# A two-layer diffusion backbone on one core: the norm barriers' elementwise work moved from GpSimd to VectorE, with the three sums on all partitions

## The chip, the core and the metric

The kernel runs on one core of one Trainium2 chip. A core has a tensor engine (TensorE, PE in the profile), a vector engine (VectorE, DVE), a scalar engine (ScalarE, ACT), GpSimd (POOL) and a sync engine (SyncE, SP) that issues most of the loads. The metric is the device time of one execution in microseconds (us), lower is better; three runs of the kernel before gave 1486.10, 1487.79 and 1488.62 us, median 1487.79.

## What is computed

Two layers of a diffusion backbone run over 256 latent tokens x and 256 context tokens, 1024 features each. Cut to what matters here:

```python
def rmsnorm(x, g):
    return x * rsqrt(mean(x * x, axis=-1) + EPS) * g

for l in range(2):
    h  = rmsnorm(x,  g_pre_mix) * (1 + sc1)  + sh1        # modulation from the conditioning vector
    hc = rmsnorm(xc, g_pre_mix) * (1 + scc1) + shc1
    y, y_ctx = token_mixer(h, hc)                         # four branches, gates, output projection
    x  = x + g1 * rmsnorm(y, g_post_mix)
    h2 = rmsnorm(x, g_pre_ffn) * (1 + sc2) + sh2
    x  = x + g2 * rmsnorm(conv_ffn(h2), g_post_ffn)
    # layer 0 does the same to the context; layer 1 needs it only as keys and values
```

Everything is fp32. The products are made of three passes over high and low parts (hi·hi, hi·lo, lo·hi), so each weight and each activation is split: the high part is a cast, the low part is the value minus the high part.

## The kernel before

**Layout.** Features lie on the 128 partitions, eight tiles `m` of 128 features; the tokens lie side by side, 512 columns of which 0 to 255 are context and 256 to 511 latent. The two halves are called streams (`streams`, `segs`); layer 1 keeps only the latent one in its second part. A dense product is `gemm_steps`: for each of eight feature tiles three matmuls (lines 236, 237, 238) into a bank of the accumulator memory (`pg` with three banks, `pa` with five).

**Weights.** `weights` loads a chunk into `st` through SP's queue and `parts` (line 215 the cast on ScalarE, line 217 the low part) splits it. The low part is VectorE's, but GpSimd's where `ahead`, `pool` or `held` says so: the first four feed-forward weights of layer 0 (`first_weights`), some of the next layer's (`tm_weights`), one of layer 1's output projection, and the three that follow a norm barrier. These last are `held`: `issue_after` puts their casts behind the last tile's ScalarE work and their low parts behind the last scaling. `stream` gives the feed-forward weights one after the other, two ahead of use; its first call issues three loads, its second makes their parts.

**A norm barrier.** It stands between two dense stages, since every feature of a token must be summed before the next product can begin. `post_tile` (lines 407 to 417) takes each output tile of the projection, multiplies it by its gain into `acc`, and keeps running sums of src², x·acc and acc². `post_sums` (line 428) adds these over the partitions by products with a matrix of ones: the first into one bank on all partitions, the two others into one bank, on partitions 0 to 31 and 32 to 63. `post_end` then computes 1/rms of the output and, from the three sums, 1/rms of the new residual without reading it again: `fold` (line 439) transposes 32x32 blocks so that a token's sum is one column, `rsqrt` (lines 318 to 327) does ten small steps, `unfold` (line 445) spreads the result back over the columns. The second root runs on 32 partitions; four copies (line 482) put it on all 128 before the last `unfold`. `scale` (line 515) multiplies `acc` by 1/rms, on GpSimd; `residual` (line 521) adds it to x, on VectorE but for tile 0; `modulate_steps` (lines 389 to 398) makes the next product's input: x·r on VectorE, two ScalarE activations for the high part and the modulated value, and the low part on VectorE.

**Order.** TensorE runs in the order of the trace. VectorE and ScalarE run in an order that a planner chooses from the trace's order, but `in_order` keeps the instructions inside it in theirs; in layer 1 that holds for the whole barrier. While the barrier lasts, TensorE is given fillers (`fill`, line 637): products of the next modulation, loaded by SP's queue. `closing` runs the last tiles a stream after the other, so that the first stream's norm runs beside the second stream's products. `channel` holds both barriers of a layer. After each barrier, `spill` stores x through GpSimd's DMA queue.

There are three barriers in the middle of the program: after the output projection of layer 0 (two streams), after its feed-forward half (two streams) and after the output projection of layer 1 (one stream). The last norm, at the very end, only scales, adds and stores (lines 1519 to 1521).

Of the kernel before, what the change touches and what calls it, by code (L numbers as in the profile page):

```python
# [18 lines left out]
D = 1024  # L19
KT = D // 128  # L20
SEQ = 256
# [12 lines left out]
# columns of the per-layer vector pack  # L34
# [4 lines left out]
# columns of the constant pack  # L39
# [114 lines left out]
class Net:  # L154
# [13 lines left out]
    # ---- allocation  # L168
# [27 lines left out]
    def weights(self, src, cols, ahead=False, pool=False, dve=False):  # L196
        return self.parts(self.staged(src, cols), cols, ahead, pool, dve)
# [6 lines left out]
    def parts(self, st, cols, ahead=False, pool=False, dve=False):  # L204
        """the high and the low part of weights"""
# [25 lines left out]
    def mm3_steps(self, out, pairs, n=None):  # L231
        """out = sum over pairs of (lhsT hi, lhsT lo, rhs hi, rhs lo): the three products that matter; yields columns streamed"""
# [12 lines left out]
    def gemm_steps(self, out, w, x, cols, k0=0, m=128, ms=128, off=0):  # L245
        """out[M, tokens] = w[:, k, M].T @ x[k][:, cols] over the k tiles of x"""
# [21 lines left out]
    def finish(self, f):  # L268
        """trace all that is queued up to f"""
# [4 lines left out]
    def gemm_tm(self, outs, x, ws, n, kg):  # L274
        """out[tokens, n] = x[k][:, tokens].T @ w[:, k, n] for several token tiles, kg k tiles to a chunk of weights"""
# [19 lines left out]
    def stack_q(self, dst, src, cols):  # L295
        """two heads of 64 features: dst[h] has a head's high parts on its own rows, its low parts on the other's"""
# [6 lines left out]
    def stack_k(self, hi, lo, src, cols):  # L303
        """hi[h] has a head's high parts on all rows; lo the low parts of both heads"""
# [7 lines left out]
    # ---- norms  # L312
    def rsqrt(self, v):
        """1/sqrt(v) by a step of third and one of second order from a guess of the exponent"""
        nc = self.nc
        stt, tt, ts = nc.vector.scalar_tensor_tensor, nc.vector.tensor_tensor, nc.vector.tensor_scalar
# [5 lines left out]
        ts(nh, v, -0.5, None, op0=ALU.mult)  # L322
        stt(t, e, -10.0 / 3.0, e, op0=ALU.add, op1=ALU.mult)  # L323
        stt(z, t, 5.0, s, op0=ALU.add, op1=ALU.mult)  # L324
        tt(a, z, z, op=ALU.mult)
        tt(b, a, nh, op=ALU.mult)
        stt(r, b, 1.5, z, op0=ALU.add, op1=ALU.mult)
        return r
# [9 lines left out]
    def sums(self, out, parts, n):  # L338
        """out[tokens, token tile] = sum over the features of all parts"""
# [8 lines left out]
    def squares(self, tiles, cols):  # L348
        """squares of the features' tiles, added in pairs"""
# [11 lines left out]
    def rstd(self, tiles, cols, room):  # L361
        """1/sqrt(mean of squares over the features + eps), on every partition, for the tokens of cols"""
# [20 lines left out]
    def modulate_steps(self, h, m, segs, r, Am, Bm, vector=False):  # L383
        """h[m] = x[m] * r * A + B, split; A and B are [128, KT, 2]; a generator that yields before the last step"""
# [15 lines left out]
    def post_tile(self, src, m, segs, G, more):  # L400
        """acc[m] = src * G, and what the norms need of it: sums of src^2, x * acc, acc^2"""
# [6 lines left out]
        for cs, b in segs:  # L408
            act = nc.scalar.activation(self.acc[:, m, cs], src[:, cs], AF.Identity, scale=G[:, m, b:b + 1])
        if more:  # L410
            act = nc.scalar.activation(yy, yg, AF.Square)
            (nc.gpsimd if m == KT - 1 and oc.start == self.xc0 else nc.vector).tensor_tensor(xy, self.xcols(m, oc), yg, op=ALU.mult)
# [5 lines left out]
        else:  # L418
            self.last3 = [t[:, oc] for t in new]
            if oc.stop == T:  # L420
                self.act = getattr(act, "ins", act)
                self.held = 3
# [1147 lines left out]
```

## Time and profile before

| | |
|---|---|
| time, median of three runs | 1487.79 us |
| span of the profiled execution | 1481.7 us |
| TensorE busy | 1399.2 us (94%) |
| VectorE busy | 983.1 us (66%) |
| ScalarE busy | 661.6 us (45%) |
| GpSimd busy | 131.8 us (9%) |
| mean granted TensorE clock | 0.971 |
| moved by DMA | 208 MB, 140 GB/s |

The profile is one execution; its span runs from the first to the last instruction, and the runs' times contain what lies around it. A busy share is an average over stages: what bounds one stage is read from the timeline and the waits of that stage. A group of instructions shows its count, the busy time of all and the mean of one, and behind the second bar the idle time before them. Matmuls overlap, so a busy TensorE can still hold less work than its window could. In a timeline a row is a start time, a length, the engine, the line, what is written and read, and in brackets the idle time before it with what ended it; equal neighbours are merged, with their count.

### The profile page before, as it was taken

What the parts mean: (1) busy time and instruction counts of PE and PEld (TensorE: products, weight loads), DVE (VectorE), ACT (ScalarE), POOL (GpSimd) and SP (SyncE); (2) the same over time, 40 slices, a digit from 0 to 9 for tenths busy, and PEclk for the clock granted to TensorE, in tenths of its full rate; (3) what the DMA queues carried; (4) which work ended last, traced back from release to release, by engine and by line L of the source; (5) the groups of instructions that cost most, each with busy time, mean ns of one, the idle gap of its engine ahead of it and who ended that gap; (6) DMA issues with size and microseconds to landing.
All of it is one profiled execution on the core that took longest, in us unless ns stands there. A gap on an engine that the chain in (4) does not pass through costs nothing. (4 is left out here: it accounts for less than half of the span.)

```text
span 1481.7 us, 22257 instructions
## 1 busy us (share of the span) xinstructions
PE 1399.2 (94%) x8657; PEld 1176.8 (79%) x8657; DVE 983.1 (66%) x1901; ACT 661.6 (45%) x1158; POOL 131.8 (9%) x136
## 2 busy tenths in 40 slices
PE   6999999999999979999999998699999999599996
PEld 3887777777778858878888887487889898599996
DVE  5458686646645797743554658958676876765666
ACT  3446444324434545323322335455563565455453
POOL 0200000100000270000000002700000000300000
PEclk8999999999999979999999999699999999799998
DMA  9722232442222624443344433453333467257553
GB/s 290 272 72 88 94 120 98 156 157 72 71 72 85 213 100 171 154 142 102 127 130 156 156 102 113 152 179 115 103 111 127 130 199 249 81 173 225 184 181 91
DMA packets 73418, 208.00 MB, mean 140 GB/s; under 512 B 6881, under 2 KB 24673, under 8 KB 73185
## 3 DMA queue, kind: packets, MB, share of 16 engines
q1 hardware_dynamic: 65792, 179.32, 37.8%
q0 software_dynamic: 7520, 27.27, 5.3%
q8 instruction: 68, 1.11, 0.3%
q14 instruction: 38, 0.30, 0.1%
HBM read 201.31 MB, written 5.24 MB: 139 GB/s over the span
## 5 line engine op out<-in xcount | busy, mean ns | idle before, releaser
L217 DVE TENSOR_TENSOR wl<-st,wh 128x1024 fp32r<-128x1024 f32 (+2 forms) x252 | 303.6, 1210 | 207.8 <-ACT wh L215 206.3
L215 ACT CAST wh<-st 128x1024 fp32r<-128x1024 f32 (+2 forms) x262 | 268.3, 1033 | 359.3 <-PE pg L237 192.7
L236 PE MATMUL pg<-hh,wh 128*128 128x512 f32 (+1 forms) x1136 | 402.6, 354 | 0.0
L238 PE MATMUL pg<-hh,wl 128*128 128x512 f32 (+1 forms) x1136 | 384.2, 338 | 1.3 <-DVE wl L217 1.2
L237 PE MATMUL pg<-hl,wh 128*128 128x512 f32 (+1 forms) x1136 | 383.3, 337 | 0.0
L236 PEld LDWEIGHTS pg<-hh,wh 128*128 128x128 f32 x1136 | 215.5, 190 | 31.4 <-issue 7.2
L238 PEld LDWEIGHTS pg<-hh,wl 128*128 128x128 f32 x1136 | 215.3, 190 | 25.9 <-DVE wl L217 2.3
L237 PEld LDWEIGHTS pg<-hl,wh 128*128 128x128 f32 x1136 | 215.7, 190 | 23.1 <-issue 3.1
L236 PE MATMUL pa<-hh,wh 128*128 128x256 f32 (+1 forms) x376 | 126.1, 335 | 1.1 <-ACT hh L292 1.1
L237 PE MATMUL pa<-hl,wh 128*128 128x256 f32 (+1 forms) x376 | 126.2, 336 | 0.6 <-DVE hl L293 0.6
L238 PE MATMUL pa<-hh,wl 128*128 128x256 f32 (+1 forms) x376 | 126.0, 335 | 0.0
L236 PE MATMUL pg<-u,wh 128*128 128x256 f32 (+1 forms) x350 | 120.2, 343 | 0.0
L237 PE MATMUL pg<-u,wh 128*128 128x256 f32 (+1 forms) x350 | 115.2, 329 | 0.0
L238 PE MATMUL pg<-u,wl 128*128 128x256 f32 (+1 forms) x350 | 115.1, 329 | 0.0
L237 PEld LDWEIGHTS pa<-hl,wh 128*128 128x128 f32 x376 | 71.4, 190 | 8.4 <-DVE hl L293 1.2
L236 PEld LDWEIGHTS pa<-hh,wh 128*128 128x128 f32 x376 | 71.4, 190 | 8.4 <-ACT hh L292 1.3
L238 PEld LDWEIGHTS pa<-hh,wl 128*128 128x128 f32 x376 | 71.4, 190 | 7.1
L236 PEld LDWEIGHTS pg<-u,wh 128*128 128x128 f32 x350 | 66.2, 189 | 12.9 <-issue 7.0
L237 PEld LDWEIGHTS pg<-u,wh 128*128 128x128 f32 x350 | 66.1, 189 | 6.5 <-issue 1.0
L238 PEld LDWEIGHTS pg<-u,wl 128*128 128x128 f32 x350 | 65.9, 188 | 6.6
L626 DVE SCALAR_TENSOR_TENSOR u<-u,cs,u 128x1024 f32<-128x1024 f32 x49 | 61.5, 1278 | 1.2 <-DMA u<-wmod 1.1
L818 ACT ACTIVATE pp<-pa,nbias 128x512 f32<-128x512 f32 (+1 forms) x48 | 29.5, 615 | 67.9 <-DVE nbias L816 37.2
(304 smaller groups left out, 2271.9 us busy)
## 6 DMA issues: line engine op xcount, KB each, us to landing
st<-wup SPq DMA_DIRECT2D x88, 512.0 KB, 3.7
st<-wgate SPq DMA_DIRECT2D x64, 512.0 KB, 3.6
u<-wmod SPq DMA_DIRECT2D x48, 512.0 KB, 4.7
u<-wmod POOLq DMA_DIRECT2D x32, 512.0 KB, 4.7
st<-wdn SPq DMA_DIRECT2D x32, 448.0 KB, 3.3
st<-win SPq DMA_DIRECT2D x26, 512.0 KB, 4.0
u<-wmod SPq DMA_DIRECT2D x32, 256.0 KB, 6.1
st<-wbr SPq DMA_DIRECT2D x16, 512.0 KB, 3.6
```

The source lines that it names most:

```text
L215: nc.scalar.copy(hi[:, :cols], st[:, :cols])
L217: (nc.gpsimd if (ahead or held or pool) and not dve else nc.vector).tensor_tensor(lo[:, :cols], st[:, :cols], hi.bitcast(F32)[:, :cols], o ...
L236: mm(out, ah, bh, start=i == 0, stop=False)
L237: mm(out, ah, bl, start=False, stop=False)
L238: mm(out, al, bh, start=False, stop=i == n - 1)
L626: nc.vector.scalar_tensor_tensor(t, st, self.cs[:, k, i:i + 1], t, op0=ALU.mult, op1=ALU.add)
L818: nc.scalar.activation(P[:, :n], S[:, :n], AF.Exp, bias=nb, scale=scale, accum_out=den)
```

## The change

All elementwise tensor work on GpSimd goes to VectorE: the low parts of weights, the scalings by 1/rms, the product x·acc of the last tile, the residual of tile 0 and a quarter of the last multiply-and-add. The holds on the weights after a barrier are removed with it. The three sums of a barrier go into three banks, each on all partitions, so that all three are folded and both roots are computed on all 128 partitions; the four copies are gone. `rsqrt` takes a list of functions (`room`) and calls one after each of its steps: the folds of the second and third sum are put into the first root, the spreading of 1/rms into the second, and in layer 1 also the scaling and the residual of tiles 0 and 1. `scale` and `add` of a tile are called together, tile by tile. In layer 1 tiles 0 and 1 are modulated with one activation on ScalarE and one instruction on VectorE in place of two activations. The second call of `stream` moves behind the modulation of both streams.

```diff
-        held = self.held > 0
-        self.held -= 1
-        with self.tc.issue_after(self.act) if held else nullcontext():
-            nc.scalar.copy(hi[:, :cols], st[:, :cols])
-        with self.tc.issue_after(self.res) if held else nullcontext():
-            (nc.gpsimd if (ahead or held or pool) and not dve else nc.vector).tensor_tensor(lo[:, :cols], st[:, :cols], hi.bitcast(F32)[:, :cols], op=ALU.subtract)
+        nc.scalar.copy(hi[:, :cols], st[:, :cols])
+        nc.vector.tensor_tensor(lo[:, :cols], st[:, :cols], hi.bitcast(F32)[:, :cols], op=ALU.subtract)
...
+    def rsqrt(self, v, room=()):
...
+        def step():
+            for f in room:
+                f()
+                break
+
         ts(y.bitcast(I32), v.bitcast(I32), -0.5, float(0x5f3759df), op0=ALU.mult, op1=ALU.add)
+        step()
         tt(a, y, y, op=ALU.mult)
         ts(s, y, 0.375, None, op0=ALU.mult)
+        step()
...
     def post_sums(self, parts, first):
         for i, p in parts:
-            o = self.s12[32 * i - 32:32 * i] if i else self.s0
-            self.nc.tensor.matmul(o[:, :p.shape[-1]], self.one[:, :o.shape[0]], p, start=first, stop=not first)
+            self.nc.tensor.matmul(self.s[i][:, :p.shape[-1]], self.one, p, start=first, stop=not first)
 
     def post_runs(self, segs):
-        self.s0, self.s12 = self.pa([T]), self.pa([T])
+        self.s = [self.pa([T]) for _ in self.run3]
...
         with self.in_order():
-            nc.vector.tensor_scalar(v, self.fold(self.s0, w), 1.0 / D, EPS, op0=ALU.mult, op1=ALU.add)
-            r = self.rsqrt(v)
-            self.unfold(r, self.rb[:, oc])
+            sums(0)
+            nc.vector.tensor_scalar(v, f[0], 1.0 / D, EPS, op0=ALU.mult, op1=ALU.add)
+            r = self.rsqrt(v, [lambda: None] * 3 + [lambda: sums(1), lambda: sums(2)] if more else ())
             if not more:
+                self.unfold(r, self.rb[:, oc])
                 return
-            s = self.fold(self.s12[0:64], w)
-            nc.vector.tensor_tensor(p[32:64], s[32:64], r[32:64], op=ALU.mult)
...
-            r2 = self.rsqrt(v2)
-            for i in range(4):
-                nc.vector.tensor_copy(r4[32 * i:32 * i + 32], r2)
-            self.unfold(r4, self.rx[:, oc])
+            nc.vector.tensor_tensor(p, f[2], r, op=ALU.mult)
+            nc.vector.scalar_tensor_tensor(q, f[1], 2.0, p, op0=ALU.mult, op1=ALU.add)
+            nc.vector.tensor_tensor(q, q, r, op=ALU.mult)
+            nc.vector.scalar_tensor_tensor(v2, q, 1.0 / D, v2, op0=ALU.mult, op1=ALU.add)
+            self.unfold(self.rsqrt(v2, [lambda: self.unfold(r, self.rb[:, oc]), *room]), self.rx[:, oc])
...
     def scale(self, m, segs):
         acc = self.acc[:, m, self.span(segs)]
-        ins = self.nc.gpsimd.tensor_tensor(acc, acc, self.rb[:, self.span(segs)], op=ALU.mult)
-        if m == KT - 1:
-            self.res = getattr(ins, "ins", ins)
+        self.nc.vector.tensor_tensor(acc, acc, self.rb[:, self.span(segs)], op=ALU.mult)
...
+    def residual(self, m, segs):
+        self.scale(m, segs)
+        self.add(m, segs)
...
                 if last:
-                    self.post_end([seg], True)
+                    self.post_end([seg], True, [lambda f=f, m=m: f(m, [seg]) for m in range(2) for f in (self.scale, self.add)])
                     self.fill(1.5)
-                if seg is segs[-1]:
-                    for m in range(KT):
-                        self.scale(m, [seg])
                 for m in range(KT):
                     if seg is not segs[-1] and m == 4:
                         self.post_end(segs[1:], True)
-                    if seg is segs[-1] or m >= 4:
-                        self.residual(m, [seg], last)
-                    open_steps.append(self.modulate_steps(h, m, [seg], self.rx, A, B))
+                    if m >= (2 if last else 4) or not last and seg is segs[-1]:
+                        self.residual(m, [seg])
+                    open_steps.append(self.modulate_steps(h, m, [seg], self.rx, A, B, last and m < 2))
...
-                    if seg is segs[0] and m == (KT - 1 if c0 == 0 else 0):
-                        next(self.ws)
                     if seg is segs[-1]:
                         self.spill(m, c0, c0)
+        next(self.ws)
         self.ffn(l, h, c0, not last)
...
-                on = nc.gpsimd if m == 4 else nc.vector
...
-                on.tensor_tensor(acc, acc, rb.to_broadcast([128, n, SEQ]), op=ALU.mult)
-                on.tensor_tensor(x, x, acc, op=ALU.add)
+                nc.vector.tensor_tensor(acc, acc, rb.to_broadcast([128, n, SEQ]), op=ALU.mult)
+                nc.vector.tensor_tensor(x, x, acc, op=ALU.add)
```

## Rows read from the trace of the kernel before

**Rows 1.** The page, part 1: busy time, share of the span, instructions.

```profile
PE 1399.2 (94%) x8657; PEld 1176.8 (79%) x8657; DVE 983.1 (66%) x1901; ACT 661.6 (45%) x1158; POOL 131.8 (9%) x136
```

**Rows 2.** Windows: length; busy PE, PEld, DVE, ACT, POOL; clock; DMA share; GB/s.

```profile
526.80:573.70 46.90, 37.62 (x273) 29.98 (x272) 38.82 (x104) 22.55 (x40) 26.38 (x20) 0.82 0.41 142
921.70:970.40 48.70, 32.62 (x164) 24.23 (x156) 41.72 (x110) 22.58 (x42) 33.23 (x33) 0.75 0.57 202
1255.20:1289.60 34.40, 18.91 (x165) 15.42 (x158) 26.15 (x61) 13.72 (x24) 14.68 (x14) 0.75 0.33 107
...
1275.00:1280.00 5.00, 4.12 (x17) 3.83 (x18) 4.18 (x13) 4.55 (x9) 0.80 (x1) 0.50 0.12 41
1280.00:1285.00 5.00, 5.00 (x41) 5.00 (x40) 3.85 (x11) 4.36 (x8) 0.76 (x1) 0.91 0.30 105
```

**Rows 3.** Timeline of TensorE, third barrier.

```profile
1275.37 0.58 PE L236 MATMUL pg<-hh,u 128*128 128x256 f32 x1 [13.85 <-ACT hh L392]
```

**Rows 4.** Timeline of VectorE, third barrier.

```profile
1256.34 0.45 DVE L439 STREAM_TRANSPOSE t<-pa 128x256 f32<-128x256 f32 x1 [3.26 <-PE pa L428]
...
1258.65 0.45 DVE L445 STREAM_TRANSPOSE rs<-n 128x256 f32<-128x256 f32 x1
...
1264.62 2.37 DVE L322 TENSOR_SCALAR n<-xms 32x8 f32<-32x8 f32 x1
...
1272.90 0.45 DVE L445 STREAM_TRANSPOSE rs<-nr 128x256 f32<-128x256 f32 x1
```

**Rows 5.** Timeline of GpSimd, third barrier.

```profile
1259.17 5.50 POOL L515 TENSOR_TENSOR acc<-acc,rs 128x256 f32<-128x256 f32 x8 [2.47 <-ACT wh L215]
1264.63 6.92 POOL L217 TENSOR_TENSOR wl<-st,wh 128x1024 fp32r<-128x1024 f32 x3
```

**Rows 6.** Groups of VectorE by line and form, first barrier, 519 to 567 us.

```profile
L482 DVE COPY nr<-n 32x8 f32<-32x8 f32 x8 | 7.7, 958 | 0.1
L389 DVE TENSOR_TENSOR t<-u,rs 128x256 f32<-128x256 f32 x16 | 7.1, 479 | 0.1
...
L521 DVE TENSOR_TENSOR u<-u,acc 128x256 f32<-128x256 f32 x14 | 5.7, 406 | 0.0
L417 DVE TENSOR_TENSOR t<-t,t 128x256 f32<-128x256 f32 x6 | 2.9, 477 | 0.1
...
L412 DVE TENSOR_TENSOR t<-u,acc 128x256 f32<-128x256 f32 x3 | 1.8, 587 | 0.1
```

**Rows 7.** Timeline of VectorE, first and second barrier.

```profile
519.39 0.45 DVE L439 STREAM_TRANSPOSE t<-pa 128x256 f32<-128x256 f32 x1 [4.30 <-PE pa L428]
...
531.78 5.98 DVE L482 COPY nr<-n 32x8 f32<-32x8 f32 x4
...
538.80 1.42 DVE L389 TENSOR_TENSOR t<-u,rs 128x256 f32<-128x256 f32 x4
...
565.75 0.92 DVE L398 TENSOR_TENSOR hl<-t,hh 128x256 fp32r<-128x256 f32 x2 [1.05 <-ACT t L396]
...
917.28 0.44 DVE L439 STREAM_TRANSPOSE t<-pa 128x256 f32<-128x256 f32 x1
...
948.81 6.44 DVE L482 COPY nr<-n 32x8 f32<-32x8 f32 x4
...
965.52 0.43 DVE L398 TENSOR_TENSOR hl<-t,hh 128x256 fp32r<-128x256 f32 x1
```

**Rows 8.** Groups, whole program: the split on VectorE and on GpSimd.

```profile
L217 DVE TENSOR_TENSOR wl<-st,wh 128x1024 fp32r<-128x1024 f32 (+2 forms) x252 | 303.6, 1210 | 207.8 <-ACT wh L215 206.3
...
L217 POOL TENSOR_TENSOR wl<-st,wh 128x1024 fp32r<-128x1024 f32 x8 | 18.7, 2345 | 47.8 <-ACT wh L215 47.8
```

**Rows 9.** Timeline of VectorE at the end of the program.

```profile
1472.26 2.36 DVE L1519 TENSOR_TENSOR acc<-acc,rs 128x512 f32<-128x512 f32 x2
...
1477.52 0.69 DVE L1520 TENSOR_TENSOR u<-u,acc 128x512 f32<-128x512 f32 x1
```

**Rows 10.** Timeline of VectorE at the start of the program.

```profile
45.90 4.36 DVE L394 TENSOR_SCALAR t<-t,A,mod 128x256 f32<-128x256 f32 x2 [1.22 <-ACT hh L392]
```

More of the change, by code (lines that the diff above doesn't have):

```diff
@@ L193, in pf, with weights @@
         return self.pa(shape) if self.turn else self.pg(shape)
-    def weights(self, src, cols, ahead=False, pool=False, dve=False):
-        return self.parts(self.staged(src, cols), cols, ahead, pool, dve)
+    def weights(self, src, cols, ahead=False):
+        return self.parts(self.staged(src, cols), cols, ahead)
     def staged(self, src, cols):
@@ L202, in staged, with parts @@
         return st
-    def parts(self, st, cols, ahead=False, pool=False, dve=False):
+    def parts(self, st, cols, ahead=False):
         nc = self.nc
@@ L408, in post_tile @@
         for cs, b in segs:
-            act = nc.scalar.activation(self.acc[:, m, cs], src[:, cs], AF.Identity, scale=G[:, m, b:b + 1])
+            nc.scalar.activation(self.acc[:, m, cs], src[:, cs], AF.Identity, scale=G[:, m, b:b + 1])
         if more:
-            act = nc.scalar.activation(yy, yg, AF.Square)
-            (nc.gpsimd if m == KT - 1 and oc.start == self.xc0 else nc.vector).tensor_tensor(xy, self.xcols(m, oc), yg, op=ALU.mult)
+            nc.scalar.activation(yy, yg, AF.Square)
+            nc.vector.tensor_tensor(xy, self.xcols(m, oc), yg, op=ALU.mult)
         if m == 0:
@@ L445, in unfold, with post_end @@
         self.nc.vector.transpose(o.rearrange("p (j r) -> p j r", r=32), r.unsqueeze(2).to_broadcast([128, J, 32]))
-    def post_end(self, segs, more):
+    def post_end(self, segs, more, room=()):
         nc = self.nc
@@ L454, in post_end @@
         small = lambda t: self.sm([16], t, bufs=1)[:, :J]
-        v, p, q, r4 = small("nv"), small("np"), small("nq"), small("nr")
-        v2 = self.xms[0:32, oc.start // 32:oc.stop // 32]
+        v, p, q = small("nv"), small("np"), small("nq")
+        v2 = self.xms[:, oc.start // 32:oc.stop // 32]
         parts = list(enumerate(self.last3))
@@ L468, in post_end, with sums @@
             self.fill(1.5)
+        f = [None] * 3
+        def sums(i):
+            f[i] = self.fold(self.s[i], w)
         with self.in_order():
[L470 to L472 removed]
+            sums(0)
+            nc.vector.tensor_scalar(v, f[0], 1.0 / D, EPS, op0=ALU.mult, op1=ALU.add)
+            r = self.rsqrt(v, [lambda: None] * 3 + [lambda: sums(1), lambda: sums(2)] if more else ())
             if not more:
+                self.unfold(r, self.rb[:, oc])
                 return
[L475 to L483 removed]
+            nc.vector.tensor_tensor(p, f[2], r, op=ALU.mult)
[3 more added lines that the diff above has]
+            self.unfold(self.rsqrt(v2, [lambda: self.unfold(r, self.rb[:, oc]), *room]), self.rx[:, oc])
     def closing(self, ws, product, segs, G, more):
@@ L504, in closing @@
                 self.post_tile(ps if product.direct else self.acc[:, m], m, [seg], G, more)
-                if i and m == KT - 2:
-                    for j in range(KT):
-                        self.scale(j, early)
         if len(segs) > 1:
@@ L514, in scale, with add @@
         acc = self.acc[:, m, self.span(segs)]
-        ins = self.nc.gpsimd.tensor_tensor(acc, acc, self.rb[:, self.span(segs)], op=ALU.mult)
-        if m == KT - 1:
-            self.res = getattr(ins, "ins", ins)
-    def residual(self, m, segs, dve=False):
+        self.nc.vector.tensor_tensor(acc, acc, self.rb[:, self.span(segs)], op=ALU.mult)
+    def add(self, m, segs):
         x = self.xcols(m, self.span(segs))
-        (self.nc.gpsimd if m == 0 and not dve else self.nc.vector).tensor_tensor(x, x, self.acc[:, m, self.span(segs)], op=ALU.add)
+        self.nc.vector.tensor_tensor(x, x, self.acc[:, m, self.span(segs)], op=ALU.add)
+    def residual(self, m, segs):
+        self.scale(m, segs)
+        self.add(m, segs)
     def in_order(self):
@@ L699, in win_steps, with tm_weights @@
         return ps
-    def tm_weights(self, l, i, ahead=False, pool=False):
+    def tm_weights(self, l, i, ahead=False):
         name, n, kg, i = ("wta", NA, KA, i) if i < 4 else ("wtb", NB, KB, i - 4)
-        return self.weights(self.A[name][l][:, kg * i * n:kg * (i + 1) * n], kg * n, ahead, pool)
+        return self.weights(self.A[name][l][:, kg * i * n:kg * (i + 1) * n], kg * n, ahead)
     def tm_start(self, h, abreast):
@@ L1302, in project @@
         for m in range(KT):
-            w = self.weights(self.A["wout"][l, m], 1024, pool=c0 > 0 and m == 1)
+            w = self.weights(self.A["wout"][l, m], 1024)
             if m >= KT - room:
@@ L1321, in first_weights @@
             self.ahead = [[] for _ in range(AHEAD)]
-        self.ahead[i // 2].append(self.weights(self.A["wup"][l, i // 2, i % 2], 1024, True, dve=l > 0))
+        self.ahead[i // 2].append(self.weights(self.A["wup"][l, i // 2, i % 2], 1024, True))
     def ffn_up(self, l, h, j, g, segs):
@@ L1425, in run @@
         self.start()
-        self.queue, self.fillers, self.owed, self.held, self.mods = [], [], 0, 0, {}
+        self.queue, self.fillers, self.owed, self.mods = [], [], 0, {}
         part = self.squares(self.x, slice(0, T))
@@ L1529, in channel @@
         for seg in segs:
-            if seg is segs[-1]:
-                for m in range(KT):
-                    self.scale(m, [seg])
             for m in range(KT):
```

17 lines of the change are left out of this document (9 added, 8 removed).

## Prediction

> **What bounds the kernel now.** I read the page's shares first: TensorE has a matmul in flight for 94% of the span, VectorE for 66%, GpSimd for 9% [rows 1]. So a change in VectorE's or GpSimd's work can only pay, or cost, where TensorE is not the one that ends last. The windows by stage show where that is: three norm barriers, after the output projection of layer 0, after the feed-forward half of layer 0 and after the output projection of layer 1. They last 46.9, 48.7 and 34.4 us and run at a mean granted clock of 0.82, 0.75 and 0.75 [rows 2]. At the full clock a 256-column product costs about 0.12 us (41 products in a 5 us window, last row but none of the group) [rows 2]. The barriers hold 192 products of 256 columns, 96 of 432 (0.2 us each by the ratio of columns) and 96 of 256, and fillers and sums, estimated at 6 or 7 us each; that is 30, 26 and 18 us of work. So about 17, 23 and 16 us are lost in them, 56 us in all, and this is what the change can win.
>
> Who ends last in a barrier is read from VectorE's own timeline. In the third barrier the first half of the norm (transpose of the sums, scaling, ten small steps) runs from 1256.34 to 1258.65, 2.3 us, while GpSimd is idle [rows 4]. The second half has fourteen steps of the same small kind, but its result is turned onto the partitions only at 1272.90 [rows 4]. In between GpSimd runs eight scalings (5.50 us from 1259.17) and three weight splits (6.92 us from 1264.63) [rows 5]: one step of 8 columns takes 2.37 us beginning at 1264.62 [rows 4], the length of one split (6.92 / 3 = 2.3). The steps advance one per GpSimd instruction. TensorE meanwhile stands still for 13.85 us [rows 3]. The first two barriers show the same: four copies of 32x8 take 5.98 us and 6.44 us [rows 7], beside GpSimd's splits. So the barriers are bound by VectorE, and VectorE by GpSimd's tensor instructions.
>
> **The change, part by part.** Prices: a 128x256 VectorE instruction follows the one before it at 0.337 us (four in 1.42 us of which the last alone is 0.41) [rows 7]; a 128x1024 split takes 1.21 us on VectorE, 2.35 us on GpSimd [rows 8]; a small step costs (2.31 - 0.45) / 11 = 0.17 us when it stands alone [rows 4], less when other work fills its gap, and I take 0.12. A transpose is taken at 0.36.
>
> That a step beside GpSimd lasts as long as GpSimd's instruction (2.37 against 2.3 us) while it takes 0.17 us alone [rows 4, 5] is why I price VectorE's work at its undisturbed rate. The Trainium skill, page "SBUF — State Buffer", section "Who interferes with whom", gives a mechanism: the two engines share a pair of ports under an exclusive lock, and the loser waits for the whole instruction. By that rule all of the stretching goes, as in the sum; but the rule also speaks against counting on a free engine, since the descriptors that GpSimd writes for its DMAs take the same lock, and no row here prices that.
>
> *Barrier 1.* Before, VectorE needs from 519.39 (first transpose) to 566.67 (last low part) [rows 7], 47.3 us. After it has: 16 products x*r and as many low parts (two streams, eight tiles), 14 additions of residuals, 6 running sums, 3 products x*acc [rows 6]; added, the 16 scalings and 2 additions that GpSimd did: 73 x 0.337 = 24.6 us. Two norms with three transposes in and two out, 10 x 0.36 = 3.6, and about 50 small steps, 6.0. The copies (7.7 us [rows 6]) are gone, since all partitions hold the sums. Together 34.2 us; the three splits of 1.2 us that were GpSimd's come to 3.6 us more but are wanted only for the third pair of feed-forward weights. If VectorE never idles, the last low part is there at 553.6, with the splits in front of it 557.2, and with 1 to 2 us of gaps 555 to 559. TensorE then has one tile left, 12 x 0.12 = 1.4 us: end at 556 to 560 against 573.7 [rows 2]. It can start early enough: the first norm needs about 7 us (worked out for barrier 3 below) instead of the 19 us from 519.39 to 538.80 [rows 7], so the products start at about 531 and their 23 us end at 554. I take 14 us; bounds 9 (7 us of further gaps) and 17 (all that is lost).
>
> *Barrier 2.* The same 34.2 us, plus three splits that the very next products need (3 x 1.0, being 864 or 1024 wide) and two additions of products to the accumulator (0.7): 37.9 us from 917.28 [rows 7], so 955.2, and 957 with gaps, against 965.95 for the last low part [rows 7]. TensorE lags less, about 1.2 us for a tile, and ends near 958 against 970.4 [rows 2]: 12 us; bounds 7 and 16.
>
> *Barrier 3.* One stream, VectorE's order written out. From 1256.34: 2.3 us for the first half; two more transposes in its gaps, +0.5; four steps, 0.8; ten steps with the spreading of r and two scalings and two additions in their gaps, 1.7 + 5 x 0.25 = 2.9; transpose out 0.45. That is 6.9 us: 1263.3 against 1273.35 [rows 4]. The first tile's residual is then done, so the first product follows 0.9 us later, 1264.2 against 1275.37 [rows 3], 11.2 us earlier. Behind it VectorE needs 4 x 0.337 = 1.35 us a tile and TensorE 12 x 0.12 = 1.4, so the gain is kept, barely. I take 11; bounds 8 (three splits in the chain's gaps, 3.4 us) and 14.
>
> *Tail.* From 1472.26 to 1478.21 VectorE does three quarters of the last multiply-and-add, GpSimd the rest; its first two take 2.36 us [rows 9]. After, eight of 512 columns at half of 1.21 us [rows 8] are 4.9 us against 5.95: 1 us; bounds 0 and 1.5.
>
> *Start.* Two scalings on VectorE take 4.36 us beside GpSimd's splits [rows 10], some 0.7 us by the widths. The 3.6 us come back less two splits, 2.2 us, that now stand on VectorE, and TensorE may have other work: 2; bounds 0 and 3.6.
>
> *Elsewhere.* Seven splits (four of the first feed-forward weights, two of the next layer's, one of the output projection) move to VectorE, 7 x 1.2 = 8.4 us. TensorE covers them where VectorE is at two thirds [rows 1]; without that cover they cost up to 8.4 us, while the stalls beside them end. I take 0; bounds -2 and +4.
>
> *Moved or widened.* The call that makes the first three streamed weights' parts moves behind the modulation. It issues no DMA (their loads went out earlier), three casts and three splits, past ScalarE's and VectorE's modulations; SP's and POOL's queues see nothing of it. The holds that put those casts behind the last tile are gone, so a cast of 1 us may delay that tile: in the bounds. Three full banks of sums have as many products as before, of the same 256 columns: 0. Of the five banks of that kind six are wanted around a barrier, so one waits for a transpose, at most 1 us, again in the bounds. Behind the barriers GpSimd has only DMAs, which now wait for VectorE's additions.
>
> Sum: 14 + 12 + 11 + 1 + 2 = 40 us off the profiled execution's span of 1481.7, 1441.7. The median of the runs, 1487.8, lies 6.1 us above that span, which I carry over: 1447.8 us. The bounds add up to 22 and 54 us, 1466 and 1434.
>
> **The rivals.**
> *VectorE takes the place of GpSimd's lock, with its order against us.* What was held is now placed freely: three splits (3.6 us) and a cast (1) inside the norm's chain, four tiles of scaling and addition (2.7 us) ahead of the first modulation, in each barrier: 7.3 x 3 = 22 us given back, 1470 us. For it: VectorE is already busy for 38.8 of 46.9 us, 41.7 of 48.7 and 26.2 of 34.4 [rows 2]. Against: much of that share is waiting.
> *The clock stays up.* In barrier 3 the products begin at half speed, 0.50 granted for 5 us after the standstill [rows 2, 3]; a shorter one may leave the clock at its upper level, worth half of 5.5 us there, and the upper bounds elsewhere: 50 us, 1438. The Trainium skill, page "TensorE: Matmul & The Clock Gate", section "What's actually happening", lets recent activity set the level; by that rule this is the likelier course, though the trace shows no such short gap here.
> *Slower.* The stretching is VectorE's own (short instructions waiting for semaphores) and stays. Then barriers 1 and 2 gain 18 instructions, two transposes and three splits, 6.1 + 0.7 + 3.6 = 10.4 us each, barrier 3 some 6.7: 27 us, 1515. It decides once less than that is recovered. Against it: the same small steps take 0.17 us with GpSimd idle and 2.37 us beside a split [rows 4, 5].
> *Nothing.* The feed-forward stage is led by its weight loads and gives the gain back: 1488. Against: DMA is busy 0.33 to 0.57 in the windows [rows 2].
>
> **How the numbers follow.** Forecast 1448 us, 0.60 (30 to 50 us won); order against us 0.23; clock stays up 0.08; nothing 0.04; slower 0.05. The range 1434 to 1472 takes in the bounds and the first two rivals. A measurement tells about 0.2% (3 us) from no change: faster 0.91, same 0.04, slower 0.05.
>
> **What would show it.** Right: in barrier 3 every small step at 0.15 to 0.2 us and the first product 7 to 8 us after the transpose of the sums; no copies; the three windows near 33, 37 and 23 us. Wrong: small steps still over 0.5 us (the lock was not the cause); 1.2 us splits between them (the first rival); VectorE at full share while TensorE waits for low parts through the second stream; new waits on weight splits in the layers' steady parts.

## The result: 36.5 us faster, and where the time came from

The changed kernel takes 1451.19 us (median, 1447.87 to 1452.06) against 1487.68 us: a ratio of 0.975, 95% interval 0.9736 to 0.9764. The forecast was 1448. Its profiled execution took 1452.06 us with a span of 1450.3, 31.4 us less than the span before.

Page, first part: busy time of each engine, share of the span, instructions (answers [rows 1]).

```profile
PE 1394.2 (96%) x8657; PEld 1177.2 (81%) x8657; DVE 957.4 (66%) x1955; ACT 663.6 (46%) x1156; POOL 36.3 (3%) x69
```

GpSimd lost 95.5 us of work. VectorE took it over, has 54 instructions more, and is busy for 25.7 us less: what it lost was stretching, and the twenty copies of 17.9 us (below).

Windows of the first two barriers, between the same products as in [rows 2], then of the first products of barrier 1 and of barrier 3.

```profile
528.93:564.14 35.21, 33.18 (x273) 28.49 (x272) 30.32 (x105) 21.92 (x38) 2.14 (x4) 0.95 0.52 189
910.48:944.13 33.65, 28.60 (x164) 19.99 (x156) 32.73 (x125) 22.75 (x41) 6.39 (x12) 1.00 0.59 213
...
536.00:541.00 5.00, 3.95 (x29) 3.06 (x30) 5.00 (x26) 3.43 (x7) 0.00 (x0) 0.74 0.89 346
...
1246.00:1251.00 5.00, 4.77 (x22) 4.77 (x23) 4.79 (x14) 2.76 (x5) 0.76 (x1) 0.50 0.19 64
1251.00:1256.00 5.00, 5.00 (x42) 5.00 (x41) 4.50 (x12) 3.85 (x7) 0.76 (x1) 0.93 0.13 46
```

46.9 us became 35.2 and 48.7 became 33.7; the granted clock of the two barriers rose from 0.82 to 0.95 and from 0.75 to 1.00. Barrier 3 still has a stretch at 0.50 behind its standstill, as before, and barrier 1 has one at 0.74.

Cut at the same products on TensorE's timeline and the first transposes on VectorE's, the two spans add up like this (us; the last column is what the sum of the prediction put there):

| stretch | before | after | difference | predicted |
|---|---|---|---|---|
| start and mixer, to barrier 1's first transpose | 519.39 | 521.42 | +2.03 | -2 |
| from there to the projection's last product | 7.27 | 7.37 | +0.10 | |
| barrier 1, to the first 512-column product | 46.31 | 34.62 | -11.69 | -14 |
| feed-forward, layer 0, to its last product | 348.31 | 346.65 | -1.66 | 0 |
| barrier 2, to the last 432-column product | 48.88 | 33.83 | -15.05 | -12 |
| layer 1: mixer and projection | 284.66 | 289.02 | +4.36 | 0 |
| barrier 3, last product to first product | 20.55 | 11.12 | -9.43 | -11 with the next |
| barrier 3, products of the first four weights | 14.36 | 15.94 | +1.58 | |
| feed-forward, layer 1, to the last norm's transpose | 179.75 | 179.36 | -0.39 | 0 |
| last norm and end | 12.22 | 10.97 | -1.25 | -1 |
| span | 1481.70 | 1450.30 | -31.40 | -40 |

Each column is one execution, and the one before was a fast one (see the item on span and median below). Where the other 5 of the 36.5 us lie, these two traces do not show.

VectorE's timeline of barrier 3 (start, duration, instruction, idle time before it), which answers [rows 4]:

```profile
1234.19 1.23 DVE L213 TENSOR_TENSOR wl<-st,wh 128x1024 fp32r<-128x1024 f32 x1 [2.72 <-ACT wh L212]
1235.33 0.42 DVE L424 TENSOR_TENSOR t<-u,acc 128x256 f32<-128x256 f32 x1
1235.67 0.44 DVE L447 STREAM_TRANSPOSE t<-pa 128x256 f32<-128x256 f32 x1
1236.14 0.17 DVE L484 TENSOR_SCALAR nv<-t 128x8 f32<-128x8 f32 x1
...
1242.02 0.45 DVE L453 STREAM_TRANSPOSE rs<-n 128x256 f32<-128x256 f32 x1
...
1244.02 0.41 DVE L406 TENSOR_SCALAR t<-t,A,mod 128x256 f32<-128x256 f32 x1 [0.58 <-ACT hh L404]
...
1245.43 0.41 DVE L406 TENSOR_SCALAR t<-t,A,mod 128x256 f32<-128x256 f32 x1 [0.67 <-ACT hh L404]
1245.76 0.42 DVE L410 TENSOR_TENSOR hl<-t,hh 128x256 fp32r<-128x256 f32 x1
```

From the first transpose to the end of the transpose out are 6.8 us (6.9 was said) instead of 17.0 [rows 4]; no small step is over 0.2 us. But a split stands right in front of the product that the sums want, and the first low part comes 3.7 us behind the transpose out, after two waits for ScalarE.

The start went the other way. VectorE's two modulations of [rows 10] are no longer stretched (0.73 us together instead of 4.36), and TensorE has new waits there (us in total, times, longest):

```profile
PE pa L232 <- ACT wh L212: 2.2, 1, 2.2
PE pa L233 <- DVE wl L213: 0.9, 1, 0.9
```

GpSimd's timeline at the start, after and, below it, before:

```profile
41.58 0.68 POOL L620 DMA_DIRECT2D u<-wmod  x1 [4.36 <-PE pa L647]
44.16 2.18 POOL L620 DMA_DIRECT2D u<-wmod  x4 [1.90 <-DMA u<-wmod]
```

```profile
50.06 2.94 POOL L610 DMA_DIRECT2D u<-wmod  x5
```

The loads of the weights wanted next, issued between 38 and 66 us (KB each, median us from issue to landing), after and before:

```profile
st<-wtb SPq DMA_DIRECT2D x2, 512.0 KB, 10.4
```

```profile
st<-wtb SPq DMA_DIRECT2D x2, 512.0 KB, 7.3
```

Rid of its two splits, GpSimd issues five loads of 512 KB from 41.6 us on instead of 50.1, and the weights that TensorE needs next land 3 us later: new waits of 2.2 and 0.9 us in place of the old one of 1.94 us for a low part. The DMA engines are full there in both kernels (from 38 to 52 us a DMA share of 1.02 before and 1.08 after), where the whole program has 0.44 and 0.45.

### The profile page after: what moved, and what is told of

It is laid out like the page before. It is cut to its first block, busy times and chain, and to the rows that moved or that the text cites. A ratio compares the mean times of both kernels' runs of the same rounds, so it can differ in the third digit from the quotient of the medians.

```text
span 1450.3 us, 22235 instructions
## 1 busy us (share of the span) xinstructions
PE 1394.2 (96%) x8657; PEld 1177.2 (81%) x8657; DVE 957.4 (66%) x1955; ACT 663.6 (46%) x1156; POOL 36.3 (3%) x69
## 4 chain that ended last, share of the span: by engine, by line
PE 74%; DVE 8%; ACT 2%; DMA 2%; issue 1%; DVEq 0%; ACTq 0%
PE pg L232 16%; PE pg L233 15%; PE pg L234 15%; PE pa L233 7%; PE pa L232 7%; PE pa L234 7%; PE pa L787 2%; DVE wl L213 1%; PE pa L817 1%; PE pa L856 1%; PE pa L840 1%; ACT wh L212 1%; PE pa L1176 1%; PE pa L647 1%; DMA u<-wmod 1%
## 5 line engine op out<-in xcount | busy, mean ns | idle before, releaser
L213 DVE TENSOR_TENSOR wl<-st,wh 128x1024 fp32r<-128x1024 f32 (+2 forms) x262 | 313.9, 1203 | 214.9 <-ACT wh L212 213.4
```

The source lines that it names most:

```text
L213: nc.vector.tensor_tensor(lo[:, :cols], st[:, :cols], hi.bitcast(F32)[:, :cols], op=ALU.subtract)
```

## The experiments

Two theories are to be told apart. Mine: VectorE's short steps wait for GpSimd's tensor instructions. The rival: they are stretched by VectorE's own order and by the copies between partitions. Each run has the kernel before beside it on its chip. Times of one kernel scatter by 2 to 9 us (1448 to 1456 for one of them), so small differences are read from the stretches of the table; line numbers shift by a few with the edits.

**Which half of the change did it.** First, all of the change but the sums (two banks, four copies of 32x8 again):

```
-            self.nc.tensor.matmul(self.s[i][:, :p.shape[-1]], self.one, p, ...
+            o = self.s12[32 * i - 32:32 * i] if i else self.s0
+            self.nc.tensor.matmul(o[:, :p.shape[-1]], self.one[:, :o.shape[0]], p, ...
```

> The changed kernel with the old form of the sums: two banks, x times acc on 32 partitions and acc squared on the next 32, and four copies of 32x8 back to all partitions; all tensor work stays on VectorE. Theory (the copies were long because of what ran on GpSimd): a copy takes 0.17 us, and with one transpose less the five norms of the barriers cost 0.3 us each more: 1452 to 1453, no difference that counts. Rival (copies between groups of partitions are long by themselves, 1.5 us each as before): 6 us for each of five norms, about 1470 to 1480.

Measured: 1453.3 us, ratio 0.9775 (0.976 to 0.9789). All twenty copies (busy us, mean ns, idle before), here and then in the kernel before:

```profile
L496 DVE COPY nr<-n 32x8 f32<-32x8 f32 x20 | 3.2, 161 | 0.2
```

```profile
L482 DVE COPY nr<-n 32x8 f32<-32x8 f32 x20 | 17.9, 894 | 0.2
```

The same copies take 0.16 us instead of 0.89. They were not long by themselves. The other half, the three banks in the kernel before with all of GpSimd's work kept:

> The kernel before with only the three banks on all partitions: no copies, all of GpSimd's scalings, splits and residuals stay. Theory: the copies only stood where a GpSimd split was running, and what stands there now is stretched as they were; 0 to 3 us for each of the five norms, of which barrier 3 shows none, 1478 to 1488 in all. Rival (the copies themselves cost): 6 us in each norm, 20 us and more in all, 1460 to 1468.

Measured: 1482.72 us, ratio 0.9973 (0.9958 to 0.9987), inside what I expected. In barrier 3 the copies are gone, and the steps on all 128 partitions are stretched as those on 32 were:

```profile
1262.83 0.64 DVE L319 TENSOR_TENSOR n<-n 128x8 f32<-128x8 f32 x1
...
1264.76 2.38 DVE L322 TENSOR_SCALAR n<-xms 128x8 f32<-128x8 f32 x1
1267.05 2.38 DVE L323 SCALAR_TENSOR_TENSOR n<-n 128x8 f32<-128x8 f32 x1
```

So 34 of the 36.5 us come without the new sums, from the engines and from what moved with them: the order of the steps, the dropped holds, the later call of `stream`. No run has the engines alone. The sums are worth 2 us on top of that, less than the runs scatter, and 4 us in the kernel before.

**One part undone.** The scalings alone back on GpSimd, in the changed kernel:

```
-        self.nc.vector.tensor_tensor(acc, acc, self.rb[...], op=ALU.mult)
+        self.nc.gpsimd.tensor_tensor(acc, acc, self.rb[...], op=ALU.mult)
```

> The changed kernel with the scalings alone back on GpSimd, wherever they now stand. VectorE has 40 instructions of 0.337 us less, 13.5 us. Theory: beside each scaling of 0.69 us VectorE advances one instruction, so what is taken off it is given back and a little more (0.69 against 0.34 + 0.34), plus the handing over from engine to engine in barrier 3, where scaling, addition and product of a tile follow one another: 1 to 4 us for each barrier, 1454 to 1463. Rival (VectorE is bound by its own count, GpSimd is a free engine): 5 us less in barriers 1 and 2, 1 us less in barrier 3, 1440.

Measured: 1464.54 us, 13.4 above the changed kernel, just over the upper end of my theory and 24.5 above the rival's. The barriers take 39.7, 38.4 and 14.3 us where they took 34.6, 33.8 and 11.1: 5 us more in each of the first two, where I had said 4 at most. GpSimd's and VectorE's timeline:

```profile
1249.48 5.94 POOL L522 TENSOR_TENSOR acc<-acc,rs 128x256 f32<-128x256 f32 x8 [80.45 <-DVE n L324]
...
1251.10 0.68 DVE L329 SCALAR_TENSOR_TENSOR n<-n 128x8 f32<-128x8 f32 x1
1251.81 0.65 DVE L331 SCALAR_TENSOR_TENSOR n<-n,n 128x8 f32<-128x8 f32 x1
```

One step per scaling again. And the three splits behind a barrier, with their casts held back as before, first on GpSimd and then, as its pair, on VectorE:

```
+        with self.tc.issue_after(self.act) if held else nullcontext():
+            nc.scalar.copy(hi[:, :cols], st[:, :cols])
+        (nc.gpsimd if held else nc.vector).tensor_tensor(lo[:, :cols], ...
```

> The changed kernel, with the three casts behind a barrier held until ScalarE is done with the last tile, and their three splits on GpSimd, in barriers 1 and 3. Its pair is the same kernel with the splits on VectorE, so what differs is the engine of six splits. Theory (VectorE waits for GpSimd's tensor instructions, which stand back to back for 3 times 2.35 us): while they run VectorE passes few of its steps; in barrier 3 the chain from the first transpose to the transpose out grows from 6.4 us to 9 to 12 us, in barrier 1 about as much, and the kernel is 4 to 10 us slower than its pair: 1453 to 1459. Rival (GpSimd takes six splits of 1.2 us off VectorE for nothing): 0 to 7 us faster than its pair, 1442 to 1449.

Measured: 1457.73 us, 7.2 above the pair's 1450.53. Barrier 3:

```profile
1238.39 6.99 POOL L216 TENSOR_TENSOR wl<-st,wh 128x1024 fp32r<-128x1024 f32 x3 [74.75 <-ACT wh L215]
...
1238.47 2.32 DVE L329 TENSOR_TENSOR n<-n,nv 128x8 f32<-128x8 f32 x1
1240.72 0.16 DVE L330 TENSOR_SCALAR n<-nv 128x8 f32<-128x8 f32 x1
1240.83 2.28 DVE L332 SCALAR_TENSOR_TENSOR n<-n 128x8 f32<-128x8 f32 x1
1243.03 0.43 DVE L451 STREAM_TRANSPOSE t<-pa 128x256 f32<-128x256 f32 x1
1243.39 2.02 DVE L334 SCALAR_TENSOR_TENSOR n<-n,n 128x8 f32<-128x8 f32 x1
```

Three splits, three steps of their length: the transpose out starts 12.5 us after the first transpose, instead of 9.5 in the pair, whose three splits stand in the chain on VectorE, and 6.35 in the changed kernel. My theory stands, the rival falls.

The two runs put 13.4 us on the scalings and 7.2 on the six splits behind barriers 1 and 3. With 2 for the sums, some 14 of the 36.5 us are left, for barrier 2's splits, the residuals and the new order of the steps together, less what the start lost; what the order alone is worth was not tried.

**The cause added back alone.** Eight GpSimd multiplies beside barrier 3's chain; the instructions of every other engine and their order are those of the changed kernel:

```
+            for _ in range(8):
+                self.nc.gpsimd.tensor_tensor(self.last3[2], self.acc[:, 7, oc], self.acc[:, 7, oc], op=ALU.mult)
```

> The changed kernel with one thing added: eight GpSimd multiplies of 128x256 that start with barrier 3's first transpose; nobody reads what they write, and every other engine has the same instructions in the same order. Theory (VectorE waits for GpSimd's tensor instructions): eight times 0.69 us, the length of such a multiply before, so for 5.5 us VectorE advances one step per multiply, 8 steps of 0.17 us that would have taken 1.4 us; the chain from the first transpose to the transpose out grows from 6.8 us to about 10.9 us, and the time by 4 us, from 1451 to 1455. Rival (short instructions are stretched by VectorE's own order and semaphores): 6.8 us stay and the time stays at 1451.

Measured: 1449.96 us (1448.03 to 1456.09), which by itself tells nothing from 1451; in the trace the chain takes 8.6 us instead of 6.35, and last product to first product 13.35 instead of 11.12. So 2.2 us, not 4 and not 0:

```profile
1238.61 5.91 POOL L480 TENSOR_TENSOR t<-acc 128x256 f32<-128x256 f32 x8 [77.02 <-PE pa L436]
...
1239.96 0.17 DVE L335 TENSOR_TENSOR n<-n,n 128x8 f32<-128x8 f32 x1
1240.16 0.47 DVE L337 SCALAR_TENSOR_TENSOR n<-n,n 128x8 f32<-128x8 f32 x1
1240.66 0.17 DVE L492 TENSOR_TENSOR np<-t,n 128x8 f32<-128x8 f32 x1
1240.87 0.47 DVE L493 SCALAR_TENSOR_TENSOR nq<-t,np 128x8 f32<-128x8 f32 x1
```

Every second step slips through: each of the short ones starts in the 0.07 to 0.08 us between the end of one multiply and the start of the next. I took these gaps for the cause, as all multiplies wrote one tile, and gave each another place:

> The changed kernel with eight GpSimd multiplies of 128x256 beside barrier 3's chain again, but now each writes another place (six places in turn), where all eight wrote the same before. That first form let VectorE pass two or three steps per multiply and cost 2.2 us in the chain where I had said 4. Theory (each multiply waited for the one before it because both wrote one tile, and VectorE slipped its steps into these gaps): now they stand back to back at about 0.69 us, VectorE passes one small step per multiply, and the chain from the first transpose to the transpose out takes 9 to 10.5 us instead of 8.6 (6.35 without them). Rival (the gaps have another reason, such as reading one operand twice): about 8.6 us again.

Measured: 1451.94 us; eight multiplies in 5.30 us, now without gaps, and a chain of 8.2 us, the rival's time. But the multiplies began at 1233.37 us, 1.2 before the first transpose, so only 4.1 us of them lay beside the chain and not the 5.5 of the sum, and the chain's length decides little. The steps tell more:

```profile
1235.75 0.53 DVE L323 TENSOR_TENSOR n<-n 128x8 f32<-128x8 f32 x1
1236.20 0.16 DVE L324 TENSOR_SCALAR n<-n 128x8 f32<-128x8 f32 x1
1236.31 0.54 DVE L326 TENSOR_TENSOR n<-n,nv 128x8 f32<-128x8 f32 x1
1236.78 0.16 DVE L327 TENSOR_SCALAR n<-nv 128x8 f32<-128x8 f32 x1
1236.89 0.54 DVE L329 SCALAR_TENSOR_TENSOR n<-n 128x8 f32<-128x8 f32 x1
```

Long and short still alternate, but only tensor_scalars with one input pass; every step with two inputs beside a multiply lasts until that multiply ends, where two-input steps had passed in the first form. So the explanation by gaps fits the steps, though not the time said for it. That the multiplies read one tile twice, where a scaling reads two and writes one of them, is a difference that was not tried.

**The start.** GpSimd's five loads held until the last low part of the start is there:

```
+        ins = nc.gpsimd.tensor_copy(late, self.lo.bitcast(F32))
+        self.late = getattr(ins, "ins", ins)
...
+                with self.tc.issue_after(self.late) if queue is nc.gpsimd else nullcontext():
+                    queue.dma_start(out=st, in_=self.A["wmod"] ...
```

> The changed kernel with GpSimd's five loads of modulation weights at the start (512 KB each) held until the last low part of the start is there, about 50 us, where GpSimd's two splits had kept them until then before. Theory (the start lost because GpSimd, free of splits, issued these loads from 41 to 46 us, and they share the DMA engines with the weights that the next products wait for): the weights land some 7 us after their issue instead of 10, TensorE's wait of 2.2 to 3.5 us for the cast and 0.7 to 0.9 us for the split goes, the first transpose of barrier 1 comes at 518 to 519.5 us instead of 521 to 523, and the time is 2 to 3 us lower, 1448 to 1449. Rival (the weights are late for another reason, the loads are themselves wanted early): first transpose at 521 or later and 1451 or more.

Measured: 1444.26 us, ratio 0.9712 (0.9697 to 0.9726), 6.9 us below the changed kernel. The loads go out from 51.39 us, the waits for the cast and the split are gone from TensorE's list, and barrier 1's first transpose comes at 515.46 us, 6.0 before the changed kernel's. Most of it arises in one place: the products that take 9.9 us from 54.0 us on in the changed kernel take 5.0 here. The two loads of 512 KB land 8.7 us after their issue, between the 7 and the 10 of the theory. The start's own first transpose moves by up to 2 us from run to run, so I count from there: to barrier 1's the changed kernel and the others with its start take 505.0 to 508.0 us, the four with the hold 499.4 to 501.3, the two with the old start 504.2 and 504.7. The hold is worth about 6 us, then; the theory had the place right and the size too small.

**Barrier 3's order.** The two modulations that VectorE does itself write a tile of their own:

```
-                nc.vector.tensor_scalar(t[:, cs], t[:, cs], a, s, op0=ALU.mult, op1=ALU.add)
+                u = self.t2([T])
+                nc.vector.tensor_scalar(u[:, cs], t[:, cs], a, s, op0=ALU.mult, op1=ALU.add)
+                t = u
```

> The changed kernel with one edit in barrier 3: the two modulations that VectorE computes itself write a tile of their own, so that they no longer wait until ScalarE has read the product x*r. Theory (the first low part comes 3.7 us after the transpose out because VectorE's written order waits twice for ScalarE, 0.58 and 0.67 us): the waits go, the first low part starts at about 2.3 us after the transpose out, everything behind it 1.3 us earlier, 1449.9. Rival: VectorE is packed behind it at 1.59 us a tile and TensorE gives the gain back by waiting for the third pair of weights: 1451.

Measured: 1448.32 us. Transpose out and first low part:

```profile
1240.82 0.45 DVE L457 STREAM_TRANSPOSE rs<-n 128x256 f32<-128x256 f32 x1
...
1243.29 0.42 DVE L414 TENSOR_TENSOR hl<-t,hh 128x256 fp32r<-128x256 f32 x1
```

2.5 us instead of 3.7, both waits gone, and barrier 3's products take 14.20 us instead of 15.94: 1.7 us by the trace. The median alone, 2.9 below the changed kernel's, lies within the scatter.

**The casts.** Held back, with the splits on VectorE (the pair above):

> The changed kernel with only the hold back on the three casts: behind ScalarE's work on the last tile; the splits stay on VectorE and stand where their casts let them. Theory (my cost of the dropped holds was too low: a cast of 1.04 us stands in front of the last tile's activations): about 1 us comes back in each of barriers 1 and 3, 1448 to 1450. Rival: VectorE is what ends last, the casts were hidden, and the splits now come later than their products want them: 1451 to 1454.

Measured: 1450.53 us, not told from the changed kernel. The same hold on top of the two edits that paid:

> The same two edits and the hold on the three casts in barriers 1 and 3. Alone the hold made 0.7 us, less than the runs scatter. Theory (a cast of 1.04 us in front of the last tile's activations is on the path): 1 to 2 us below the kernel with two edits. Rival (ScalarE's delay is hidden or paid back later by the third pair of weights): the same time within 1 us.

Measured: 1441.72 us against 1441.54 without it: nothing, as the rival had it, but not because the casts were hidden. Layer 1's mixer and projection take 285.58 us with the hold and 287.57 without, 2.0 less (1.1 of it in the projection's last 14 products, the rest earlier, where such differences come and go from run to run), and the way from the last product to the first one 13.00 instead of 11.12, 1.9 more. With the casts later, all three splits fall into the chain:

```profile
1222.39 2.93 ACT L215 CAST wh<-st 128x1024 fp32r<-128x1024 f32 x3
...
1223.74 1.22 DVE L216 TENSOR_TENSOR wl<-st,wh 128x1024 fp32r<-128x1024 f32 x1
...
1225.78 1.21 DVE L216 TENSOR_TENSOR wl<-st,wh 128x1024 fp32r<-128x1024 f32 x1
1226.91 0.16 DVE L338 TENSOR_TENSOR n<-n,n 128x8 f32<-128x8 f32 x1
1226.98 1.22 DVE L216 TENSOR_TENSOR wl<-st,wh 128x1024 fp32r<-128x1024 f32 x1
```

Holding the splits behind the transpose out as well was not tried.

**Both edits together.**

> The changed kernel with the two edits that paid, together: GpSimd's five loads at the start held, and a tile of its own for the two modulations in barrier 3. They lie 700 us apart, so their gains should add: 1451.2 less 6.9 (measured for the first alone) less 2.9 (for the second alone, of which its trace explains 1.7) is 1441.4, or 1442.6 by the trace. If the first one's gain was partly chance (its trace explains 6.0, of which some 0.6 to 2 lie before the first norm's transpose, where no instruction differs), 1444.

Measured: 1441.54 us, ratio 0.9706 (0.969 to 0.9722); the gains add. With its twin that has the hold (1441.72) it is the fastest kernel here, 9.7 us below the change. In its profiled execution barrier 1 takes 32.71 us instead of 34.62, though no instruction differs there and VectorE needs the same 36.5 us from the first transpose to the last low part. What differs is the granted clock, here in the same stretch, 16 to 20 us behind that transpose, of the changed kernel and, below it, of this one:

```profile
537.42:541.42 4.00, 3.73 (x23) 3.32 (x24) 4.00 (x21) 2.46 (x5) 0.00 (x0) 0.62 0.96 384
```

```profile
530.78:534.78 4.00, 4.00 (x37) 3.59 (x38) 4.00 (x20) 2.46 (x5) 0.00 (x0) 1.00 0.99 390
```

A mean of 0.62 is partly the lower of the two levels (1.2 GHz), 1.00 the upper (2.4 GHz) throughout, and TensorE begins 37 matmuls there instead of 23. In the 4 us before, it had been busy for 2.23 and 2.35 us.

**The other splits.** On that kernel, five of the seven splits away from the barriers back on GpSimd:

> The kernel with two edits, and five of the seven splits that lie away from the barriers (four of the first feed-forward weights of layer 0, one of the output projection of layer 1) back on GpSimd. My sum put their move to VectorE at 0, bounds a gain of 2 and a cost of 4. If TensorE covers VectorE there, the two kernels are equal within 1 us. If VectorE's queue is what ends last there, this one is 2 to 4 us faster; if GpSimd's lock stretches VectorE's steps in the steady part, up to 2 us slower.

Measured: 1445.01 us (1440.37 to 1446.15), ratio 0.9722 (0.9703 to 0.9741), which overlaps its pair's. A zero in the sum is not refuted; if there is a difference, VectorE is the better place for them. Layer 1's 4.4 us do not come back with it (289.6 us for that stretch).

## Why the prediction was right, and where its sum was not

- *What bounds the barriers.* Right. Putting either kind of GpSimd work back brings the stretched steps back, with the durations named, and the copies are short without it. The Trainium skill, page "SBUF — State Buffer", section "Who interferes with whom", adds that VectorE contends when it reads two operands from SBUF, or in a two-port mode, and not with one input outside such a mode. The runs agree as far as they go: the transpose from PSUM at 1243.03 keeps its 0.43 us where a split begins, between steps of 2.28 and 2.02 us that read two, and in the kernel before with three banks another (0.41 us at 1259.48) runs inside a scaling. The tensor_scalar of 2.38 us and the copies of 0.89 us have one input and would have to be in such a mode, which no run here shows. The runs add that eight GpSimd multiplies with gaps between them cost the chain 2.2 us, of the 4 that I had worked out from back-to-back ones.
- *Barrier 1, 14 predicted, 11.7 measured.* From the first transpose to the last low part VectorE took 36.5 us; my 34.2 and the three splits in front make 37.8, so VectorE's terms were right. What failed is "TensorE then has one tile left": it ended 5.5 us behind that low part, not 1.4. Its products began 16.8 us behind the first transpose where I had 11.6, and at a granted clock of 0.62 for the first 4 us. The clock is worth some 1.5 us: with the two edits it stayed at 1.00 and the products took 23.6 us instead of 25.2. Why they began 5 us late is open. Fillers that waited for loads (1.17 and 0.86 us) are part of it; the three casts before the second stream's last tiles hardly are, since with the casts held the products begin 16.2 and 16.6 us behind the transpose.
- *Barrier 2, 12 predicted, 15.05 measured.* My count of 37.9 us for VectorE was 3 too long, and the granted clock was 1.00 where it had been 0.75: here the second rival came true. The upper bound of 16 held.
- *Barrier 3, 11 predicted, 7.85 measured (9.43 less 1.58).* The chain was as worked out (6.8 for 6.9 us), though the first product came 8.4 us behind the transpose of the sums, not the 7 to 8 named as the sign. Two steps failed: the dropped hold put a cast and a split in front of the sums (first transpose 2.8 us behind the last product instead of 1.5, and 1.5 again in the run with two edits and the hold), which I had in the bounds at 1 us; and "the gain is kept, barely" overlooked that two modulations in place wait for ScalarE's reading of the same tile, 1.7 us by the run that gave them their own. The lower bound of 8 was just missed.
- *Start, 2 gained predicted (3.6 less 2.2 is 1.4, put at 2), 2.0 lost,* outside the bounds of 0 to 3.6; 1.2 of the 2.0 lie before the start's own first transpose, within its scatter. The stall went as said. What failed is that I asked what the faster engine does for the waiting one and not what it triggers: the splits had been holding back five loads. I had seen for another edit that "SP's and POOL's queues see nothing of it"; for this one I did not look at POOL's queue. Without the collision the term is a gain of 3 to 5 us by the counts above (504.2 or more, against 499.4 to 501.3).
- *Elsewhere, 0 predicted, 2.3 lost* (+4.36, -1.66, -0.39). Of layer 1's 4.36, 1.2 us are the dropped hold: the projection's last 14 products take 3.1 to 3.3 us in the nine kernels without it and 2.0 to 2.1 in the five with it. The other 3.1 can't be put down to the change. Up to these products the stretch takes 282.6 us in the kernel before, but 285.8 in the same kernel with only the three banks, which keeps all of GpSimd's work, and 283.5 to 286.4 in the kernels with the change: single executions that differ by waits of TensorE for splits and casts, mostly in the merge.
- *Tail, 1 predicted, 1.25 measured.* Right.
- *From span to median.* This step failed, and helped, which was luck. The changed kernel's profiled run took 1.76 us more than its span, not 6.1, so the old kernel's profiled execution, 1481.7 us long, will have taken about 1483.5: an execution at the fast end of a scatter of 1482 to 1492. The sum promised 8.6 us too much of the span; this gave back 4.3, another 0.9 is the profiled run's place above its median, and 3.4 us of error are left. The bounds were added with a slip as well: 9, 7 and 8 less the cost of 4 elsewhere make 20 us, not 22.
- *The rivals.* The first, casts and splits in the chain, was real, but some 2.4 us around barrier 3 (1.2 in the projection's last products, 1.2 in front of the sums), not 7.3 in each. The second came true in barrier 2, in barrier 1 in some executions (0.95 over the window of the changed kernel's, 1.00 from the first product on with the two edits), not in barrier 3. The third and the fourth fell, though the fourth's mechanism, loads that lead, decided the start.

## What to carry to other kernels

Price a chain of short VectorE steps by what runs on GpSimd at that moment: one long two-input instruction there can cost one step its whole length, however small the step is. When work leaves an engine, look at what stood queued behind it there, DMAs above all, since they will start earlier and may meet the loads that are wanted next. And take the distance from span to time from a run that shows both, not from a profiled span and another run's median.

## What was not expected of the hardware

Steps beside GpSimd are stretched by very different amounts: 2.0 to 2.4 us beside 128x1024 splits, 0.65 beside scalings of two tiles, and 0.47 to 0.57 beside multiplies of 0.6 us, for every second one only where these leave gaps of 0.07 us. And five loads of 512 KB issued some 9 us earlier cost about 6 us, in a kernel whose DMA share is 0.45 on average: they fell into the start, where it is full.
